# A hybrid SSD, attention and expert layer on one core: the SSD's mask, exponentials and products spread over steps, and the first LayerNorm done in halves

## The chip, the core and the metric

The kernel runs on one core of a Trainium2 chip. The metric is the device time of one execution in microseconds; the kernel before took 1722.3 us (median of three executions, 1720.65 to 1722.61). Shares and rows come from one profiled execution. The engines are TensorE (PE; its weight loads are PEld), VectorE (DVE), ScalarE (ACT), GpSimd (POOL) and SyncE (SP), which here issues most DMAs. Each works through its own queue in order.

## The reference, cut to what matters

512 rows of width 1024 pass through one decoder layer:

```python
h = layer_norm(x, ln_in_g, ln_in_b)
proj = h @ w_in                                   # z, xbc, dt, q_lat, kv_lat, k_pe
xbc = silu(causal_dwconv(xbc, conv_w, conv_b))    # 4 taps; then xs, B, C
seg = a_cum[..., :, None] - a_cum[..., None, :]
decay = exp(where(causal, seg, -inf))
y_diag = einsum('bcgels,bcsgep->bclgep', cb[:, :, :, None] * decay, xdt)
# states between chunks, y_off = C . prev . exp(a_cum), y += d_skip * xs, gate by silu(z)
# in parallel: latent attention of 8 heads; both @ w_out; LayerNorm; expert mixer; LayerNorm
```

There are 16 SSD heads of width 64 in two groups with a state of 128. The kernel works with chunks of 128 rows (c = 0 to 3), so that chunk and group (c, g) make eight pieces of eight heads, each a 128 x 8 x 128 tile of decays. All matrix products of the projections are made of three passes (high times high, high times low, low times high) of operands that are split into a high and a low half.

## The kernel before, in words

The order of all instructions is written by hand: what is issued first in the Python text stands first in its engine's queue. Buffers come from pools, and a tile that reuses a buffer makes its writer wait for the old readers.

**Weights.** `Stream` (L75 to L108) brings the weights as numbered items of 512 KB. `loads` issues a DMA on SP into one of three raw buffers `wir`; `splits` makes the high half `wih` on ScalarE (L99) and the low half `wil = wir - wih` (L100) on the engine that `lo` names, VectorE as a rule, and then issues the load three items on. `get(n)` splits up to item n + 2; there are three pairs of `wih` and `wil`. `proj(i)` (L294) takes item i and does 8 blocks k of three matmuls (`mm3`, L66 to L69) over 512 columns into a psA bank of PSUM. psA and psB have four banks each.

**First LayerNorm** (L228 to L280). The four row blocks of `XH` are loaded; statistics of all four, one `rsqrt` (a bit trick and three Newton steps on VectorE, L110), one scale `nm4`; the blocks are normalised by ScalarE and VectorE; then for each of eight column blocks k four transposes on TensorE into a bank, `ht` on ScalarE (gain and bias), the high half `HH` by a copy on VectorE and the low half `HL` on VectorE for even k and on GpSimd for odd k. Then `XH` times gain plus bias (L276, L277; the rows come by a broadcast DMA `rows`, L235) makes the residual, three blocks on GpSimd and one on VectorE, stored to `xsp` by DMAs of GpSimd's queue. The low half of item 0 is made on GpSimd too.

**Projections of the SSD** (L515 to L533). For i = 0 to 12: `proj(i)`; `conv_a` (ScalarE's copy `cu`, four VectorE steps into `ca`), a step later `conv_b` (SiLU on ScalarE), and two steps later `conv_c` (four transposes on TensorE, a copy on ScalarE; nothing for i = 3 and 4). The dt path (`dt_prep`) runs in pieces between; its last piece writes the cumulated decays `acT` to memory (`acd`), and `decay_rows(n)` reads them back by a broadcast DMA of GpSimd's queue into one of three `de` tiles, the next when `ssd_y` has used one. `k_rope` (i = 3) has two fp32 matmuls.

**SSD.** `ssd_a(c, g)` (L406): for g = 0 the product C·B of the chunk on TensorE, in a psB bank, and ScalarE's copy `cbT`; then the mask on VectorE (L415), eight exponentials on ScalarE (L418) and the product with `cbT` on VectorE (L419). `ssd_x(c)`: `xdt`, `xdw` and the skip product on VectorE. `ssd_off(c)`: two matmuls with the state, and on VectorE `yo` (L441) and its sum (L442). `ssd_y(c, g)`: 8 fp32 matmuls of 128 x 128 (L450) in two psB banks, emptied by VectorE sums (L454). `ssd_s(c)`: the state (L464, L461, L466). The table `work` puts these behind the projections 13 to 17 (q and kv latents, steps 0 to 4) and the eight gate items (z, L588, steps 5 to 12). `lat_a` and `lat_b` (L550, L563) normalise the latents: column sums, an `rsqrt` chain, a diagonal, a matmul, scales and splits.

**Attention** (from L765): `q_pe(0)` and `qk_nope(0)`, then three steps of `chain(qk_nope(1), v_proj(0))`, the third of which is the first half of `v_proj(0)`; then 38 steps `st` with scores, softmax, transposes and products, each taking one more step of the chain.

Behind it come the output projection, a LayerNorm, the expert scores, and the long expert stage (`ut` and `v` items) that takes most of the time. The change does not touch them.

Of the kernel before, what the change touches and what calls it, by code (L numbers as in the profile page):

```python
# [23 lines left out]
S = 512  # L24
# [24 lines left out]
def tile_block(ctx: ExitStack, tc: tile.TileContext, I, out):  # L49
# [119 lines left out]
    def rows(t, i):  # L169
        nc.sync.dma_start(t, bass.AP(tensor=I["rows"].tensor, offset=I["rows"].offset + i * D,  # L170
                                       ap=[[0, 128], [D, 2], [1, D]]))
# [51 lines left out]
    def item():  # L223
        cnt[0] += 1
        return win.get(cnt[0] - 1)
# [5 lines left out]
    win.loads(1)  # L231
# [10 lines left out]
    nc.sync.dma_start(iaE.rearrange("p a b -> p (a b)"), I["ch"][:, 256:512])  # L242

    V.memset(ones, 1.0)
    win.lo = lambda n: G if n == 0 else lo_on[0]
    win.splits(1)
    mv4 = lnp.tile([128, NB, 2], F32, name="mv4")
    ve4 = lnp.tile([128, NB], F32, name="ve4")
    for b in range(NB):
        st6 = lnp.tile([128, 2, 6], F32, name="st6", bufs=2)  # L250
        for i in range(2):
            V.bn_stats(st6[:, i], XH[:, b, i * 512:(i + 1) * 512])
        V.bn_aggr(mv4[:, b], st6.rearrange("p a b -> p (a b)"))
    V.tensor_scalar(ve4, mv4[:, :, 1], EPS, None, op0=OP.add)
    rs4 = rsqrt(lnp, ve4, [128, NB], "l0")
    nm4 = lnp.tile([128, NB], F32, name="nm4")
    V.scalar_tensor_tensor(nm4, mv4[:, :, 0], -1.0, rs4, op0=OP.mult, op1=OP.mult)
    for b, cs, act in ((0, slice(0, D), 0), (1, slice(0, D), 1), (2, slice(0, D), 0),
                       (3, slice(0, 512), 1), (3, slice(512, D), 0)):
        t = XH[:, b, cs]  # L260
        if act:
            A.activation(t, t, AF.Identity, bias=nm4[:, b:b + 1], scale=rs4[:, b:b + 1])
        else:
            V.tensor_scalar(t, t, rs4[:, b:b + 1], nm4[:, b:b + 1], op0=OP.mult, op1=OP.add)
    for k in range(8):
        ps = pa() if k % 2 else pb()
        for b in range(NB):
            T.transpose(ps[:, b * 128:(b + 1) * 128], XH[:, b, k * 128:(k + 1) * 128], ident)
        ht = lnp.tile([128, S], F32, name="ht", bufs=3)
        A.activation(ht, ps, AF.Identity, bias=PAR[:, P_LB + k:P_LB + k + 1], scale=PAR[:, P_LG + k:P_LG + k + 1])  # L270
        V.tensor_copy(HH[:, k], ht)
        (G if k % 2 else V).tensor_tensor(HL[:, k], ht, HH[:, k], op=OP.subtract)
    win.splits(3)
    for b in range(NB):
        E = V if b == 3 else G
        E.tensor_tensor(XH[:, b], XH[:, b], zt[:, 0], op=OP.mult)  # L276
# [14 lines left out]
    kpe = [lat.tile([128, S], F32R, name=f"kpe{i}") for i in range(2)]  # L291
    kd = wk.tile([128, S], F32, name="kd")

    def proj(i):  # L294
        h, l = item()
        h = h.rearrange("p (k c) -> p k c", k=8)
        l = l.rearrange("p (k c) -> p k c", k=8)
        ps = pa()
        for k in range(8):
            mm3(ps, h[:, k], l[:, k], HH[:, k], HL[:, k], k == 0, k == 7)  # L300
        return ps

    cu, co = {}, {}
# [51 lines left out]
    def dt_prep():  # L355
# [33 lines left out]
        for n in range(3):  # L389
            decay_rows(n)  # L390
        ps = pb()
        T.matmul(ps[:, 0:64], tri, af, start=True, stop=True)
# [13 lines left out]
    def ssd_a(c, g):  # L406
        sl = slice(c * 128, (c + 1) * 128)
        if g == 0:
            pc = pb()
            for e in range(2):  # L410
                T.matmul(pc[:, e * 128:(e + 1) * 128], bcT[:, e, sl], bcT[:, 2 + e, sl], start=True, stop=True)
            cbT = SD["cb"] = ssw.tile([128, 2, 128], F32, name="cbT")
            A.activation(cbT.rearrange("p a b -> p (a b)"), pc[:, :256], AF.Copy)
        de = de_[c * 2 + g]
        V.tensor_tensor(de, de, ntm[:, None, :].to_broadcast([128, 8, 128]), op=OP.add)  # L415
        for h in range(8):
            hh = g * 8 + h
            A.activation(de[:, h], de[:, h], AF.Exp, bias=nac[:, c, hh:hh + 1])  # L418
        V.tensor_tensor(de, de, SD["cb"][:, g:g + 1].to_broadcast([128, 8, 128]), op=OP.mult)  # L419

    def ssd_x(c):
        xdt = SD["xdt"] = ssw.tile([128, D], F32, name="xdt")
# [11 lines left out]
    def ssd_off(c):  # L434
        if c:
            for g in range(2):
                po = pb()
                T.matmul(po, bcT[:, 2 + g, c * 128:(c + 1) * 128], prev[0][:, g * 512:(g + 1) * 512],
                         start=True, stop=True)
                yo = ssw.tile([128, 512], F32, name="yo")  # L440
                V.tensor_tensor(hb(yo), hb(po), eac[:, c, g * 8:(g + 1) * 8, None].to_broadcast([128, 8, 64]), op=OP.mult)  # L441
                V.tensor_tensor(xs[g][:, c], xs[g][:, c], yo, op=OP.add)  # L442

    def ssd_y(c, g):
# [8 lines left out]
            yv = y[:, q % 2 * 256:(q % 2 + 1) * 256].rearrange("p (a b q) -> p a b q", a=2, b=2)  # L453
            V.tensor_tensor(yv, yv, pv, op=OP.add)  # L454
        del de_[c * 2 + g]
        decay_rows(c * 2 + g + 3)

    def ssd_s(c):
        nxt = ssw.tile([128, D], F32, name="prev", bufs=2)
# [82 lines left out]

# [876 lines left out]
```

## Time and profile before

| | |
|---|---|
| median of three executions | 1722.3 us |
| the profiled execution | 1720.65 us |
| its span, first to last instruction | 1718.9 us |
| TensorE busy | 1631.2 us (95%) |
| VectorE busy | 1373.3 us (80%) |
| ScalarE busy | 680.2 us (40%) |
| GpSimd busy | 484.5 us (28%) |
| TensorE clock granted, mean | 0.986 |

A row of the timeline has the start, the length, the engine, the line, the operation, output and inputs, and in brackets the idle time before it and what ended it. A row of the groups has the count (x8), then busy time and mean ns of one, then idle time before it. Matmuls overlap, so the distance of their starts, not their length, is the rate. A row of the windows has a stretch, its length, the busy time of PE, PEld, DVE, ACT and POOL, the granted clock (1.00 or 0.50 within one stretch), the DMA share and GB/s.

### The profile page before, as it was taken

Reading aid. Unit: us, or ns where it says so; the run is one execution under the profiler, and the core shown is the slowest. Engines: PE = TensorE matmul, PEld = TensorE weight load, DVE = VectorE, ACT = ScalarE, POOL = GpSimd, SP = SyncE. Lnnn points to the kernel's source line nnn. Section 1 sums busy time; section 2 is a strip of 40 time slices with the busy share of each in tenths; the row PEclk is TensorE's granted clock in tenths of the full one; section 3 lists DMA queues with packets and bytes.
Section 4 is the critical chain, followed back from the end, with each engine's and each line's share of the span. In section 5 each row is a group of like instructions: output and inputs, shape, how many; then the busy total and the mean of one; then the engine's idle time right before and its main releaser. Section 6 shows DMA issues by size and latency. Waiting matters only on the chain.

```text
span 1718.9 us, 23562 instructions
## 1 busy us (share of the span) xinstructions
PE 1631.2 (95%) x8639; PEld 1432.0 (83%) x8639; DVE 1373.3 (80%) x2659; ACT 680.2 (40%) x1072; POOL 484.5 (28%) x331
## 2 busy tenths in 40 slices
PE   5998899999899989999999999999999999999996
PEld 4776677878788989898989999999999999888884
DVE  8877678864639999999668778787788888898976
ACT  3463456652223333555433333333333333333331
POOL 5100000000033410000045455555444544643301
PEclk9999999999999999999999999999999999999998
DMA  5333111265322333666689999999999999999972
GB/s 193 115 112 109 51 51 42 79 228 158 121 77 86 99 99 122 233 221 233 235 304 334 321 344 330 317 335 336 340 308 346 334 318 332 348 348 335 335 219 100
DMA packets 145491, 384.66 MB, mean 224 GB/s; under 512 B 11856, under 2 KB 62032, under 8 KB 143456
## 3 DMA queue, kind: packets, MB, share of 16 engines
q1 hardware_dynamic: 104672, 236.85, 40.6%
q0 software_dynamic: 40416, 145.80, 23.6%
q8 instruction: 67, 1.10, 0.3%
q10 hardware_dynamic: 288, 0.52, 0.1%
q14 instruction: 48, 0.39, 0.1%
HBM read 350.59 MB, written 31.49 MB: 222 GB/s over the span
## 4 chain that ended last, share of the span: by engine, by line
PE 71%; DVE 19%; ACT 5%; issue 2%; DMA 1%; DVEq 0%; SPq 0%; ACTq 0%
PE va L1175 10%; PE va L1176 10%; PE va L1179 10%; PE pu L67 8%; PE pu L69 8%; PE pu L68 8%; DVE wil L100 3%; PE pa L67 2%; PE pa L68 2%; PE pa L69 2%; ACT wih L99 2%; PE pw L69 2%; PE pw L68 2%; PE pw L67 2%; DVE t L883 1%
## 5 line engine op out<-in xcount | busy, mean ns | idle before, releaser
L100 DVE TENSOR_TENSOR wil<-wir,wih 128x1024 fp32r<-128x1024 f32 (+3 forms) x314 | 378.9, 1208 | 207.2 <-ACT wih L99 204.3
L99 ACT ACTIVATE wih<-wir 128x1024 fp32r<-128x1024 f32 (+2 forms) x340 | 352.4, 1038 | 330.9 <-issue 162.3
L69 PE MATMUL pu<-XTH,wil 128*128 128x384 f32 x1008 | 341.4, 339 | 4.4 <-DVE wil L100 4.4
L67 PE MATMUL pu<-XTH,wih 128*128 128x384 f32 x1008 | 344.0, 341 | 1.0 <-ACT sc L869 1.0
L68 PE MATMUL pu<-XTL,wih 128*128 128x384 f32 x1008 | 340.9, 338 | 0.0
L1212 POOL DMA_INDIRECT row<-u,ix x128 | 190.6, 1489 | 434.8 <-DMA wir<-v 261.8
L1175 PE MATMUL va<-wih,Ph 128*128 128x512 f32 x768 | 300.5, 391 | 2.1 <-ACT Ph L1159 2.1
L1176 PE MATMUL va<-wil,Ph 128*128 128x512 f32 x768 | 300.5, 391 | 0.3 <-DVE wil L100 0.3
L1212 POOL DMA_INDIRECT row<-v,ix x128 | 183.6, 1434 | 202.0 <-DVE ac L1229 172.8
L1179 PE MATMUL va<-wih,Pl 128*128 128x512 f32 x768 | 239.4, 391 | 0.0
L1066 ACT ACTIVATE act<-pu 128x384 f32<-128x384 f32 x126 | 62.0, 492 | 366.8 <-PE pu L69 366.8
L69 PEld LDWEIGHTS pu<-XTH,wil 128*128 128x128 f32 x1008 | 189.1, 188 | 5.0 <-DVE wil L100 5.0
L67 PEld LDWEIGHTS pu<-XTH,wih 128*128 128x128 f32 x1008 | 189.1, 188 | 4.0 <-ACT sc L869 1.2
L68 PEld LDWEIGHTS pu<-XTL,wih 128*128 128x128 f32 x1008 | 189.3, 188 | 2.9
L1175 PEld LDWEIGHTS va<-wih,Ph 128*128 128x128 f32 x768 | 144.6, 188 | 31.7 <-ACT Ph L1159 2.8
L1179 PEld LDWEIGHTS va<-wih,Pl 128*128 128x128 f32 x768 | 144.4, 188 | 30.5 <-DVE Pl L1166 0.3
L1176 PEld LDWEIGHTS va<-wil,Ph 128*128 128x128 f32 x768 | 144.5, 188 | 28.9 <-DVE wil L100 0.7
L1229 DVE SCALAR_TENSOR_TENSOR ac<-row,hd,ac 128x1024 f32<-128x1024 f32 x128 | 164.1, 1282 | 2.3
L1223 DVE SCALAR_TENSOR_TENSOR row<-row,x 128x1024 f32<-128x1024 f32 x128 | 150.0, 1220 | 0.8 <-DMA row<-u,ix 0.8
L100 POOL TENSOR_TENSOR wil<-wir,wih 128x1024 fp32r<-128x1024 f32 x26 | 62.4, 2401 | 233.3 <-ACT wih L99 233.3
L1151 DVE TENSOR_TENSOR P<-act,gt 128x384 f32<-128x384 f32 x128 | 70.6, 552 | 6.4 <-DMA gt<-gsp 6.4
L1159 ACT ACTIVATE Ph<-P 128x384 fp32r<-128x384 f32 x128 | 65.9, 515 | 20.5 <-DVE P L1151 20.4
(397 smaller groups left out, 2494.6 us busy)
## 6 DMA issues: line engine op xcount, KB each, us to landing
wir<-ut SPq DMA_DIRECT2D x128, 512.0 KB
wir<-v SPq DMA_DIRECT2D x128, 512.0 KB
gsp<-stg SPq DMA_DIRECT2D x12, 2048.0 KB
gt<-gsp SPq DMA_DIRECT2D x32, 768.0 KB
wir<-wo SPq DMA_DIRECT2D x26, 512.0 KB
wir<-wf SPq DMA_DIRECT2D x18, 512.0 KB
wir<-wqr SPq DMA_DIRECT2D x16, 512.0 KB
de<-acd POOLq DMA_DIRECT2D x8, 512.0 KB
```

The lines of the kernel that those rows point to most:

```text
L67: T.matmul(ps, lh, rh, start=start, stop=False)
L68: T.matmul(ps, lh, rl, start=False, stop=False)
L69: T.matmul(ps, ll, rh, start=False, stop=stop)
L99: A.activation(h, r, AF.Copy)
L100: self.lo(n).tensor_tensor(l, r, h, op=OP.subtract)
L1151: V.tensor_tensor(P.rearrange("p (b t) -> p b t", t=32), a.rearrange("p (b t) -> p b t", t=32), gt[c // 4][:, :, c % 4, :], op=OP.mult)
L1175: T.matmul(va[b][e], Ph[:, bs], h[:, cs], start=c == 0, stop=False)
L1176: T.matmul(va[b][e], Ph[:, bs], l[:, cs], start=False, stop=False)
L1179: T.matmul(va[b][e], Pl[:, bs], h[:, cs], start=False, stop=c == 127)
L1212: G.indirect_dma_start(out=R[s], out_offset=None, in_=I["u"] if s < 128 else I["v"], in_offset=bass.IndirectOffsetOnAxis(ap=ix[:, s % 128: ...
L1223: V.scalar_tensor_tensor(r, r, 1.0, x3, op0=OP.mult, op1=OP.mult, accum_out=hd[:, s:s + 1])
L1229: V.scalar_tensor_tensor(ac, r, hd[:, s - 128:s - 127], ac, op0=OP.mult, op1=OP.add)
```

## The change

1. **LayerNorm in two halves.** Statistics, `rsqrt`, scale, normalising and transposes are done for blocks 0 and 1, then for 2 and 3, into eight open PSUM banks. ScalarE makes both blocks of the first half. Then per k: `ht` on ScalarE; `HH` on ScalarE from PSUM for odd k, on VectorE for even k; `HL` always on VectorE. The low half of item 0, and the residual of all four blocks, are on VectorE.
2. **Loads.** Items 0 to 2 are asked for earlier. The broadcast `rows` moves from the head of SP's queue to behind the split of item 1.
3. **Two projections in step.** Items 0 and 1 run block by block through two banks; `get` goes on with item 2.
4. **`conv_c` later** for the first ones: 1 at step 4, and 3 and 2 at step 5.
5. **SSD.** The mask becomes `ssd_m`, issued one place before the exponentials, and those one place before the sums that use them; `ssd_a` for g = 0, with the C·B product, now often stands right behind `ssd_y`. Four `de` tiles instead of three. `acT` and `yo` lose their own buffers and use the two `cu` buffers.
6. **Attention.** Two steps of the chain ahead of the loop instead of three.

```diff
-    rows(zt[:, 0:2], 0)
-
-    win.loads(2)
+    win.loads(3)
...
+    PS8 = [pa() if k < 4 else pb() for k in range(8)]
+    for p in range(2):
+        bs = slice(2 * p, 2 * p + 2)
...
+        rs = rsqrt(lnp, ve, [128, 2], "l0")
+        V.scalar_tensor_tensor(nm, mv4[:, bs, 0], -1.0, rs, op0=OP.mult, op1=OP.mult)
...
+        for k in range(8):
+            for b in (2 * p, 2 * p + 1):
+                T.transpose(PS8[k][:, b * 128:(b + 1) * 128], XH[:, b, k * 128:(k + 1) * 128], ident)
     win.splits(1)
...
+        A.activation(ht, PS8[k], AF.Identity, bias=pl, scale=pg)
+        if k % 2:
+            A.activation(HH[:, k], PS8[k], AF.Identity, bias=pl, scale=pg)
         else:
+            V.tensor_copy(HH[:, k], ht)
+        V.tensor_tensor(HL[:, k], ht, HH[:, k], op=OP.subtract)
+        if k == 0:
+            win.splits(2)
+            rows(zt[:, 0:2], 0)
     win.splits(3)
     for b in range(NB):
-        E = V if b == 3 else G
-        E.tensor_tensor(XH[:, b], XH[:, b], zt[:, 0], op=OP.mult)
-        E.tensor_tensor(XH[:, b], XH[:, b], zt[:, 1], op=OP.add)
+        V.tensor_tensor(XH[:, b], XH[:, b], zt[:, 0], op=OP.mult)
+        V.tensor_tensor(XH[:, b], XH[:, b], zt[:, 1], op=OP.add)
...
+    def proj_k(ps, hl, k):
+        h, l = (z.rearrange("p (k c) -> p k c", k=8)[:, k] for z in hl)
+        mm3(ps, h, l, HH[:, k], HL[:, k], k == 0, k == 7)
...
+                for k in range(8):
+                    for j in range(2):
+                        proj_k(two[j], win.w[j], k)
...
-            t = de_[n] = ssw.tile([128, 8, 128], F32, name="de", bufs=3)
+            t = de_[n] = ssw.tile([128, 8, 128], F32, name="de", bufs=4)
...
-        acT = ssw.tile([64, 128], F32, name="acT")
+        acT = wk.tile([128, S + 3], F32, name="cu", bufs=2)[0:64, 0:128]
...
-        V.tensor_tensor(de, de, ntm[:, None, :].to_broadcast([128, 8, 128]), op=OP.add)
...
+    def ssd_m(c, g):
+        de = de_[c * 2 + g]
+        V.tensor_tensor(de, de, ntm[:, None, :].to_broadcast([128, 8, 128]), op=OP.add)
...
-                yo = ssw.tile([128, 512], F32, name="yo")
+                yo = wk.tile([128, S + 3], F32, name="cu", bufs=2)[:, :512]
...
-        if i >= 3:
+        if i >= 5:
             conv_c(i - 2)
+        if i in (4, 5):
+            conv_c(i - 3)
...
+        if i == 11:
+            ssd_m(0, 0)
         if i == 12:
+            ssd_m(0, 1)
             ssd_a(0, 0)
...
-    work = {0: [(conv_c, 12), (ssd_x, 0)], 1: [(ssd_y, 0, 0), (ssd_y, 0, 1)],
-            2: [(ssd_s, 0), (ssd_a, 1, 0)], 3: [(ssd_a, 1, 1), (ssd_x, 1), (ssd_off, 1)],
-            4: [(ssd_y, 1, 0), (ssd_y, 1, 1)], 5: [(ssd_s, 1), (ssd_a, 2, 0)],
-            6: [(ssd_a, 2, 1), (ssd_x, 2), (ssd_off, 2)], 7: [(ssd_y, 2, 0), (ssd_y, 2, 1)],
-            8: [(ssd_s, 2), (ssd_a, 3, 0)], 9: [(ssd_a, 3, 1), (ssd_x, 3), (ssd_off, 3)],
+    work = {0: [(conv_c, 12), (ssd_x, 0), (ssd_m, 1, 0)],
+            1: [(ssd_y, 0, 0), (ssd_y, 0, 1), (ssd_a, 1, 0), (ssd_m, 1, 1)],
+            2: [(ssd_s, 0), (ssd_a, 1, 1), (ssd_m, 2, 0)], 3: [(ssd_x, 1), (ssd_off, 1), (ssd_m, 2, 1)],
+            4: [(ssd_y, 1, 0), (ssd_y, 1, 1), (ssd_a, 2, 0)], 5: [(ssd_s, 1), (ssd_a, 2, 1), (ssd_m, 3, 0)],
+            6: [(ssd_x, 2), (ssd_off, 2), (ssd_m, 3, 1)], 7: [(ssd_y, 2, 0), (ssd_y, 2, 1), (ssd_a, 3, 0)],
+            8: [(ssd_s, 2), (ssd_a, 3, 1)], 9: [(ssd_x, 3), (ssd_off, 3)],
             10: [(ssd_y, 3, 0), (gate, 0, 0)], 11: [(ssd_y, 3, 1), (gate, 1, 0), (gate, 2, 0)],
             12: [(gate, 3, 0)]}
...
-    for _ in range(3):
+    for _ in range(2):
         next(g)
```

More of the change, by code (lines that the diff above doesn't have):

```diff
@@ L230, in tile_block @@
     nc.sync.dma_start(PAR, I["fpar"])
-    win.loads(1)
+    win.loads(2)
     nc.sync.dma_start(CT, I["cst1"])
@@ L244, in tile_block @@
     V.memset(ones, 1.0)
-    win.lo = lambda n: G if n == 0 else lo_on[0]
-    win.splits(1)
[L247 to L262, printed above, removed]
-        else:
-            V.tensor_scalar(t, t, rs4[:, b:b + 1], nm4[:, b:b + 1], op0=OP.mult, op1=OP.add)
@@ L265, in tile_block @@
[L265 to L272, printed above, removed]
+    mv4 = lnp.tile([128, NB, 2], F32, name="mv4")
@@ new lines, in tile_block @@
+    PS8 = [pa() if k < 4 else pb() for k in range(8)]
+    for p in range(2):
+        bs = slice(2 * p, 2 * p + 2)
+        for b in (2 * p, 2 * p + 1):
+            st6 = lnp.tile([128, 2, 6], F32, name="st6", bufs=2)
+            for i in range(2):
+                V.bn_stats(st6[:, i], XH[:, b, i * 512:(i + 1) * 512])
+            V.bn_aggr(mv4[:, b], st6.rearrange("p a b -> p (a b)"))
+        ve = lnp.tile([128, 2], F32, name="ve", bufs=2)
+        nm = lnp.tile([128, 2], F32, name="nm", bufs=2)
+        V.tensor_scalar(ve, mv4[:, bs, 1], EPS, None, op0=OP.add)
+        rs = rsqrt(lnp, ve, [128, 2], "l0")
+        V.scalar_tensor_tensor(nm, mv4[:, bs, 0], -1.0, rs, op0=OP.mult, op1=OP.mult)
+        for j, cs, act in (((0, slice(0, D), 1), (1, slice(0, D), 1)) if p == 0 else
+                           ((0, slice(0, D), 0), (1, slice(0, 512), 1), (1, slice(512, D), 0))):
+            t = XH[:, 2 * p + j, cs]
+            if act:
+                A.activation(t, t, AF.Identity, bias=nm[:, j:j + 1], scale=rs[:, j:j + 1])
+            else:
+                V.tensor_scalar(t, t, rs[:, j:j + 1], nm[:, j:j + 1], op0=OP.mult, op1=OP.add)
+        for k in range(8):
+            for b in (2 * p, 2 * p + 1):
+                T.transpose(PS8[k][:, b * 128:(b + 1) * 128], XH[:, b, k * 128:(k + 1) * 128], ident)
@@ L292, in tile_block @@
     kd = wk.tile([128, S], F32, name="kd")
+    def proj_k(ps, hl, k):
+        h, l = (z.rearrange("p (k c) -> p k c", k=8)[:, k] for z in hl)
+        mm3(ps, h, l, HH[:, k], HL[:, k], k == 0, k == 7)
+    two = {}
     def proj(i):
-        h, l = item()
-        h = h.rearrange("p (k c) -> p k c", k=8)
-        l = l.rearrange("p (k c) -> p k c", k=8)
+        if i < 2:
+            if i == 0:
+                cnt[0] = 2
+                for j in range(2):
+                    two[j] = pa()
+                for k in range(8):
+                    for j in range(2):
+                        proj_k(two[j], win.w[j], k)
+            return two[i]
+        hl = item()
         ps = pa()
         for k in range(8):
-            mm3(ps, h[:, k], l[:, k], HH[:, k], HL[:, k], k == 0, k == 7)
+            proj_k(ps, hl, k)
         return ps
@@ L385, in dt_prep @@
         T.matmul(ps[0:64, 0:128], af, tri, start=True, stop=True)
-        acT = ssw.tile([64, 128], F32, name="acT")
+        acT = wk.tile([128, S + 3], F32, name="cu", bufs=2)[0:64, 0:128]
         A.activation(acT, ps[0:64, 0:128], AF.Copy)
         G.dma_start(acd, acT)
-        for n in range(3):
+        for n in range(4):
             decay_rows(n)
@@ L455, in ssd_y @@
         del de_[c * 2 + g]
-        decay_rows(c * 2 + g + 3)
+        decay_rows(c * 2 + g + 4)
     def ssd_s(c):
```

2 lines of the change are left out of this document (added).

## The prediction

> **What bounds the kernel now.** I read the page first, then the waits of TensorE in the stretch that the change touches (20 to 275 us), then the groups of VectorE from 110 to 232 us, then stretches with the granted clock.
>
> ```profile
> span 1718.9 us, 23562 instructions
> ...
> PE 71%; DVE 19%; ACT 5%; issue 2%; DMA 1%; DVEq 0%; SPq 0%; ACTq 0%
> ```
>
> TensorE carries 71% of the chain that ended last. The change leaves its matmuls alone, so it can only move the waits between them, and all of it lies ahead of 260 us. What it gains there shifts all that follows, since each later stage reads the one before.
>
> ```profile
> PE pb L450 <- ACT wih L99: 7.1, 1, 7.1
> PE pb L332 <- ACT bcT L323: 3.1, 1, 3.1
> PE pb L332 <- ACT co L323: 2.2, 2, 1.9
> PE pa L68 <- POOL HL L272: 2.2, 2, 1.5
> PE pt L735 <- DVE P L726: 2.1, 1, 2.1
> PE pb L450 <- ACT ca L580: 1.7, 1, 1.7
> PE pb L565 <- DVE xs L454: 1.6, 1, 1.6
> ...
> PE pb L450 <- issue: 1.5, 1, 1.5
> ...
> PE pb L450 <- DVE yo L441: 0.9, 2, 0.4
> ```
>
> These are all the TensorE waits worth naming: 5.3 us in LayerNorm and the first convolutions (L68, bcT), 15.0 us in the SSD (L450, L565, co), 2.1 us in the first attention step.
>
> ```profile
> L100 DVE TENSOR_TENSOR wil<-wir,wih 128x1024 fp32r<-128x1024 f32 x11 | 13.4, 1219 | 0.3 <-ACT wih L99 0.3
> L419 DVE TENSOR_TENSOR de<-de,cbT 128x1024 f32<-128x1024 f32 x8 | 9.8, 1225 | 21.7 <-ACT de L418 21.7
> ```
>
> VectorE stands still for 21.7 us in 110 to 232 us, each time between its mask (L415) and its product (L419), for eight exponentials. What TensorE waits for comes behind that.
>
> ```profile
> 47.37:50.78 3.41, 0.30 (x3) 0.31 (x4) 3.41 (x2) 0.99 (x2) 2.97 (x3) 1.00 0.04 16
> 50.78:57.61 6.83, 6.83 (x14) 3.47 (x13) 3.82 (x9) 2.19 (x4) 0.00 (x0) 0.50 0.65 224
> 115.64:119.05 3.41, 1.55 (x10) 1.05 (x9) 2.36 (x2) 3.38 (x8) 0.00 (x0) 1.00 0.00 0
> 119.05:122.46 3.41, 3.41 (x11) 2.64 (x10) 0.00 (x0) 3.40 (x9) 0.00 (x0) 0.50 0.00 0
> ```
>
> First column after the length is TensorE's busy time, the third from the right the clock. A stretch with 1.55 of 3.41 us busy is followed by 3.41 us at half clock, one with 0.30 busy by 6.83 us. Half clock over 3.41 us costs 1.7 us of matmuls.
>
> **A. LayerNorm, two projections, residual (to about 55 us).**
>
> ```profile
> 11.50 2.33 DVE L117 SCALAR_TENSOR_TENSOR l0a<-l0y 128x4 f32<-128x4 f32 x1
> ...
> 14.84 0.16 DVE L257 SCALAR_TENSOR_TENSOR nm<-mv,l0y 128x4 f32<-128x4 f32 x1
> ...
> 18.83 0.69 DVE L272 TENSOR_TENSOR HL<-ht,HH 128x512 fp32r<-128x512 f32 x1
> ```
> ```profile
> L270 ACT ACTIVATE ht<-pb,PAR 128x512 f32<-128x512 f32 x4 | 3.1, 779 | 1.9 <-POOL HL L272 1.3 <-PE pb L268 0.6
> ...
> L276 DVE TENSOR_TENSOR XH<-XH,zt 128x1024 f32<-128x1024 f32 x1 | 3.4, 3424 | 0.0
> ...
> L99 ACT ACTIVATE wih<-wir 128x1024 fp32r<-128x1024 f32 x6 | 6.2, 1052 | 8.3 <-DMA wir<-wf 8.3
> ```
>
> While GpSimd works, VectorE's 0.16 us step takes 2.33 and its 1024-wide one 3.42 instead of about 1.22 (L100 above). The change takes all GpSimd arithmetic out of here. The second `rsqrt` chain costs 13 more steps at 0.2 (13.83 to 14.84 holds five), 2.5 us, and saves that 2.2 us stall, so the last scale `nm` comes at 15.1 us, as now (14.84 + 0.16). From there ScalarE has 0.8 (half block), three splits at 1.05, and eight `ht` plus four `HH` at 0.78: 13.3 us, less about 0.08 of overlap per operation: done at 27.3. VectorE's share (per pair of blocks one cast and two differences of 0.69) fits beside it, and a matmul needs only its own block k.
>
> ```profile
> 150.44 0.39 PE L68 MATMUL pa<-HL,wih 128*128 128x512 f32 x1
> 150.66 0.39 PE L69 MATMUL pa<-HH,wil 128*128 128x512 f32 x1
> ```
>
> Matmuls start every 0.227 us. The two projections in step are held for the second block until HL1 (15.1 + 0.8 + 1.05 + 0.78 + 1.05 + 2 x 0.78 + 0.69, about 21.1); then 7 x 6 x 0.227 = 9.5: both end at 30.6, item 2 (24 x 0.227 = 5.45) at 36.0.
>
> Now the price. Eight residual steps stand on VectorE ahead of the first convolution and of the low half (wil) of item 3. They were never seen alone; bounds are 1.22 each (L100, two f32 operands, same size) and 3.42 (beside GpSimd). GpSimd is idle, so I take 1.22, 1.15 start to start.
>
> ```profile
> 51.46 0.55 DVE L312 TENSOR_SCALAR ca<-cu,PAR 128x512 f32<-128x512 f32 x1 [0.55 <-ACT wih L99]
> 52.04 2.33 DVE L314 SCALAR_TENSOR_TENSOR ca<-cu,PAR,ca 128x512 f32<-128x512 f32 x3
> ```
>
> 27.3 + 1.2 (wil of item 2) + 8 x 1.15 + 3.1 (convolution 1) + 1.2 = 42.0. TensorE, done with item 2 at 36.0, has the small dt transposes and item 3's first two matmuls (no wil in them) and then waits about 5.2 us: longer than the 3.1 us wait on bcT that the later `conv_c` removes. Item 3 then ends at 42.0 + 22 x 0.227 = 47.0.
>
> ```profile
> 50.48 0.86 PE L332 MATMUL pb<-ident,bcT 128*128 128x128 f32 x4 [3.14 <-ACT bcT L323]
> 51.27 2.07 PE L508 MATMUL pb<-kd,CT 64*128 64x512 f32 x2
> ...
> 54.98 0.79 PE L67 MATMUL pa<-HH,wih 128*128 128x512 f32 x1
> ```
>
> `k_rope` (51.27 to 54.98) takes 3.7 at half clock, 1.9 at full: item 4 at 48.9, plus 1.7 to 3.4 for the clock after so long a wait, say 2.6: 51.5. Now it starts at 54.98 and loses another 1.3 until 57.61. Gain 4.8; the moved transposes (0.86 at half clock) still have to be paid, 0.4. **A: -4.4**, from -7.0 (no half clock) to -3.6.
>
> **B. SSD (109 to 232 us).** In times of the present trace, up to item 12's end (109) nothing differs.
>
> ```profile
> 111.27 1.28 ACT L418 ACT_TABLE_LOAD   x1
> 114.09 2.45 ACT L418 ACTIVATE de<-de,nac 128x128 f32<-128x128 f32 x8 [1.54 <-DVE de L415]
> ```
>
> (1) The mask is done an item earlier, so these exponentials start 1.54 sooner; the co wait falls from 1.9 to 0.3 and its half-clock stretch (119.05) goes: 3.2 us. But ScalarE's queue, only 1.5 us ahead, now rules: the first `ssd_y` starts about 124.3 instead of 126.12.
>
> ```profile
> 126.12 3.74 PE L450 MATMUL pb<-xdt,de 128*128 128x128 f32 x32
> 129.61 0.48 PE L67 MATMUL pa<-HH,wih 128*128 128x512 f32 x1
> ```
> (2) A new wait. The next chunk's C·B product now stands right behind `ssd_y` and takes the fifth of four psB banks: it waits for the first L454, which stands in VectorE's queue behind xdt's second half, xdw, the skip products, a mask, a wil and a sum (0.6 + 1.15 + 1.2 + 1.15 + 1.15 + 0.65 = 5.9). TensorE ends `ssd_y` at 127.8, gets its bank at 130.5 and starts item 15 at 130.9, not 129.61. Everything on TensorE is queued behind this wait, and so are ScalarE's exponentials, behind the copy of that product.
>
> (3) From here VectorE no longer stands still in front of xdt. TensorE: item 15 to 136.4, chunk state 1.7, item 16 to 143.6, the sums of `lat_a` 0.8. VectorE (1.15 start to start for a 1024-wide step, 0.7 for a 512-wide one, as HL) gets its last exponentials of chunk 1 at 141.1 (behind ScalarE's copies of the state) and has product, mask and wil done at 144.6; then the rsqrt chain with its diagonal 2.4 + 0.9, xdt, xdw and skip 3.5, y_off 4 x 0.7, mask, wil and sum 2.9, and L454 of chunk 1 0.4: 157.5. The waits 1.7 + 1.5 + 0.9 + 1.6 become one of 2.5 (`ssd_y` ends at 154.9), and behind the product `lat_b` (L565) starts at 157.9.
>
> ```profile
> 160.55 0.70 PE L565 MATMUL pb<-co,ones 128*128 128x512 f32 x1 [1.57 <-DVE xs L454]
> ```
> ```profile
> 171.72 0.88 DVE L560 TENSOR_SCALAR co<-ident,lsy 128x128 f32<-128x128 f32 x4
> ```
>
> (4) From the product of chunk 2 (160.8) VectorE is the bound without a pause: product 1.2, `lat_b` 3 x 2.1 (two steps and ScalarE's copy between), wil 1.2, rsqrt and diagonal 3.3, state 2.5, product, mask and wil 3.5, `lat_b` 2 x 2.1, xdt, xdw and skip 3.5, y_off 2.9, mask and wil 2.3, L454 0.4 are 31.3 us, to 192.1. The 7.1 us wait splits into waits of 1.1, 0.8, 1.6, 1.8, 0.6 and 2.5, and the fourth gate item starts at 192.5, with chunk 3's product (0.4) already behind it. Now:
>
> ```profile
> 196.91 0.48 PE L67 MATMUL pa<-wih,HH 128*128 128x512 f32 x1
> ```
>
> Gain 196.91 - 192.5 + 0.4 = 4.8. After that neither kernel waits until 232 us. Against it: the new waits of 2.7 and 2.5 us leave stretches emptier than 115.64 did. If they fall so (I say 7 in 10), each costs 1.7: 2.4. (The one at 155 us would be hidden under VectorE.) **B: -2.4**, from -4.8 to +2.0 (two double stretches, 3.4 each).
>
> The Trainium skill ("TensorE: Matmul & The Clock Gate", section "HAM oscillation — how this bites in real kernels") states that only idle gaps above about 3.4 us throttle; by it B would be -4.8. The trace differs: waits of 3.14 and 1.85 us were throttled.
>
> **C. First attention steps.** `v_proj` is begun a step later.
>
> ```profile
> 247.61 0.60 ACT L637 ACTIVATE vh<-pu 128x512 fp32r<-128x512 f32 x1 [1.53 <-PE pu L69]
> ```
>
> The first exponential need no longer wait for the second half of v: 1.1 us sooner, but vl (0.69) then falls into the softmax chain. **C: -0.8**, from 0 to -2.1 (the whole L735 wait).
>
> At nothing I cost the fourth `de` buffer (its load goes out with the first three and is used a chunk later; wrong, it would hold mask and VectorE by its landing), the copies in `cu` slots (no convolution is left when `yo` takes one), and the residual's stores (earlier, on a POOL queue that is else idle).
>
> Sum: 4.4 + 2.4 + 0.8 = 7.6 off the profiled execution's 1720.65 (span 1718.9 and 1.75 around it): 1713.05. That execution is the fastest of three; the median stands 1.65 above it, so 1714.7.
>
> **Rivals.** *B gives nothing* (VectorE's queue order eats it; for it, the new bank waits; against, the 21.7 us that are filled): 1722.3 - 5.2 = 1717.1. *No new half clock in B* (for it, the new waits are shorter than the 3.14 that was throttled; against, 1.85 was too): 1714.7 - 2.4 = 1712.3; the Trainium skill's rule above is this case. *The clock takes it all*: every new wait, those at 37, 128, 155 and 190 us, is followed by 6.83 us at half clock as 47.37 was: A loses 0.8 more, B 3 x 3.4 - 2.4 = 7.8, C is nothing: 1714.7 + 9.4 = 1724.1, no change. *Slower: the gain and bias rows come late.*
>
> ```profile
> 7.33 0.33 SPq L170 DMA_DIRECT2D zt<-rows  x1
> ```
>
> This 1 MB load now stands on SP behind the loads of items 3 and 4, which wait for wil of items 0 and 1 (about 20.5 us). Up to 28.5 us it is hidden; then each us holds the residual steps, the in-order VectorE, item 3 and TensorE. From 36.1 it eats the whole gain, from 39.6 on the kernel is slower; at 41, 1727. Against it:
>
> ```profile
> 0.00:20.00 20.00, 4.09 (x17) 3.51 (x18) 13.63 (x32) 6.58 (x7) 2.60 (x6) 1.00 0.85 317
> ```
>
> At 317 GB/s, 1.5 MB take 5 us: 26.
>
> **Chances.** Forecast 0.52, no new half clock 0.2, B nothing 0.15, clock 0.08, rows late 0.05. A measurement tells about 0.2% (3.4 us) from no change. Faster (below 1718.9): 0.52 + 0.2 + 0.1 = 0.82; same: 0.08 + 0.05 = 0.13; slower 0.05. Range: down to 1708 (A -7.0, B -4.8, C -2.1), up to 1719.5 (A -3.6, B +0.8, C 0).
>
> **What would show it.** Right: no GpSimd arithmetic before 60 us, both first projections done near 31, a new TensorE wait on wil L100 of about 5 us near 37 to 42; the 21.7 us in front of the product nearly gone, new waits of about 2.6 us before the C·B products, each on L454 or its like. Wrong: residual steps well above 1.22 us, half clock after most new waits, or L450 still waiting 5 us or more.

## The result, and the profile after

| | before | after |
|---|---|---|
| median | 1722.45 us (1720.65 to 1723.21, 4 runs) | 1709.67 us (1709.52 to 1710.38, 4 runs) |
| profiled execution | 1720.65 us | 1709.54 us |
| its span | 1718.9 us | 1707.6 us |

The ratio is 0.9928 (95% interval 0.9911 to 0.9945): 12.8 us faster, where 7.6 was forecast. Profile against profile it is 11.1 us. First the page, then the waits of TensorE from 20 to 232 us (total, times, longest):

```profile
span 1707.6 us, 23555 instructions
...
PE 71%; DVE 20%; ACT 5%; issue 2%; DMA 1%; DVEq 0%; SPq 0%; ACTq 0%
```
```profile
PE pb L430 <- DVE xs L476: 6.6, 3, 2.4
PE pa L69 <- DVE wil L100: 4.8, 1, 4.8
PE pb L472 <- issue: 2.8, 2, 1.7
PE pb L472 <- DVE xdt L448: 1.3, 1, 1.3
PE pb L460 <- DVE prev L488: 0.8, 1, 0.8
PE pb L351 <- ACT co L342: 0.7, 2, 0.4
```

The chain has the same owners as before. The 7.1 us wait on wih and the 3.1 on bcT are gone, and the two new kinds that the forecast named stand on top: the C·B product (L430) three times on a bank that L476 must free, and item 3 on its low half (L100).

To place the gain I set the same instruction of both kernels side by side on TensorE: the C·B product of chunk 0 (before, then after), the start of the latent attention (MLA, the first product of `q_pe`), and a softmax scale (VectorE) well inside the attention.

```profile
109.56 0.61 PE L411 MATMUL pb<-bcT 128*128 128x128 f32 x4
...
236.02 1.02 PE L653 MATMUL pu<-qx,C 128*128 128x512 f32 x2
...
317.98 0.49 DVE L726 TENSOR_SCALAR P<-P,sm 128x512 f32<-128x512 f32 x1
```
```profile
104.70 0.61 PE L430 MATMUL pb<-bcT 128*128 128x128 f32 x4
...
226.48 1.02 PE L681 MATMUL pu<-qx,C 128*128 128x512 f32 x2
...
307.61 0.49 DVE L754 TENSOR_SCALAR P<-P,sm 128x512 f32<-128x512 f32 x1
```

| part | forecast | measured |
|---|---|---|
| A, to 109 us | -4.4 | 109.56 to 104.70: -4.86 |
| B, to the start of MLA | -2.4 | -9.54 in all: -4.68 |
| C, first attention steps | -0.8 | -10.37 in all: -0.83 |
| behind it | 0 | span -11.26 in all: -0.9 |

A and C came as forecast; B brought twice as much; the last 0.9 comes in a part of the code that is the same in both. In the windows of the kernel before there is a stretch at half clock (0.50) that the changed one does not have at that place, and half of 3.41 us is 1.7:

```profile
368.23:371.64 3.41, 1.50 (x8) 0.91 (x7) 1.99 (x3) 2.49 (x3) 0.00 (x0) 1.00 0.61 208
371.64:375.05 3.41, 3.41 (x9) 2.65 (x10) 0.97 (x1) 0.00 (x0) 0.00 (x0) 0.50 0.96 297
```

Windows of the changed kernel, around the wait on wil and around the first wait on L476:

```profile
35.78:39.19 3.41, 1.24 (x8) 0.62 (x6) 3.20 (x6) 1.88 (x2) 0.80 (x2) 1.00 0.38 154
39.19:46.02 6.83, 4.18 (x10) 3.31 (x11) 6.57 (x10) 1.58 (x2) 0.00 (x0) 0.50 0.61 203
121.10:124.51 3.41, 2.15 (x20) 1.96 (x18) 3.41 (x5) 0.00 (x0) 1.05 (x2) 1.00 0.51 169
124.51:127.93 3.42, 2.27 (x12) 1.96 (x13) 2.09 (x6) 1.52 (x6) 0.00 (x0) 1.00 0.81 241
...
46.02:247.41 201.39, 184.99 (x895) 146.61 (x893) 146.96 (x261) 103.42 (x204) 5.85 (x11) 1.00 0.26 83
```

The wait on wil draws 6.83 us at half clock, as forecast; 4.18 us of them have matmuls, so about 2 us are lost. None of the three new SSD waits draws any: the clock stays at 1.00 from 46.02 to 247.41.

### The profile page after: what moved, and what is told of

It reads as the page before. It is cut to its first block, busy times and chain, and to the rows that moved or that the text cites. A ratio compares the mean times of both kernels' runs of the same rounds, so it can differ in the third digit from the quotient of the medians.

```text
span 1707.6 us, 23555 instructions
## 1 busy us (share of the span) xinstructions
PE 1625.9 (95%) x8639; PEld 1427.6 (84%) x8639; DVE 1364.7 (80%) x2678; ACT 682.7 (40%) x1077; POOL 458.6 (27%) x320
## 4 chain that ended last, share of the span: by engine, by line
PE 71%; DVE 20%; ACT 5%; issue 2%; DMA 1%; DVEq 0%; SPq 0%; ACTq 0%
PE va L1204 10%; PE va L1203 10%; PE va L1207 10%; PE pu L67 8%; PE pu L69 8%; PE pu L68 8%; DVE wil L100 3%; PE pa L69 2%; PE pa L67 2%; PE pa L68 2%; PE pw L69 2%; PE pw L68 2%; PE pw L67 2%; ACT wih L99 1%; DVE t L911 1%
## 5 line engine op out<-in xcount | busy, mean ns | idle before, releaser
L100 DVE TENSOR_TENSOR wil<-wir,wih 128x1024 fp32r<-128x1024 f32 (+2 forms) x315 | 376.8, 1198 | 209.1 <-ACT wih L99 206.6
L100 POOL TENSOR_TENSOR wil<-wir,wih 128x1024 fp32r<-128x1024 f32 x25 | 60.0, 2401 | 221.0 <-ACT wih L99 221.0
```

What stands on the lines that cost most here:

```text
L100: self.lo(n).tensor_tensor(l, r, h, op=OP.subtract)
```

## The experiments

My theory of the extra 2.3 us of B: the new waits are as long as forecast, but whether one draws a half-clock stretch depends on where it falls in the clock's 3.41 us stretches (the phase of the clock, for short), so the 2.4 us that I charged were the wrong size. The rival is that B saved more waiting than I counted. For A, the theory was that the residual on VectorE is what TensorE waits for. Times are compared with the kernel before on the same chip.

**e1_ln_alone and e2_ssd_alone: the parts by themselves.** The first is the changed kernel with old SSD order and attention, the second the kernel before with these lines:

```diff
+    def ssd_m(c, g):
+        de = de_[c * 2 + g]
+        V.tensor_tensor(de, de, ntm[:, None, :].to_broadcast([128, 8, 128]), op=OP.add)
...
+            1: [(ssd_y, 0, 0), (ssd_y, 0, 1), (ssd_a, 1, 0), (ssd_m, 1, 1)],
...
+            t = de_[n] = ssw.tile([128, 8, 128], F32, name="de", bufs=4)
```

> Part A alone (LayerNorm in halves, two projections in step, residual on VectorE, later conv_c); SSD order and attention as before. Theory (the gains of the parts add, what is left is read from the trace): item 12 ends 4.9 us sooner (110.17 to 105.3), the SSD keeps its 15 us of waits, the whole is 4.9 us shorter: 1717.5 beside 1722.4. Rival (part A's gain hangs on the SSD behind it, or on the clock's stretches falling otherwise): item 12 as said, but the whole shorter by 3 us or less, or by 7 or more, with the difference in half-clock stretches behind 110 us.

> Part B alone (masks, exponentials and products a step apart, four row buffers, the two borrowed buffers); everything ahead of 110 us and the attention as before. Theory 1 (the new waits of 2.1 to 2.4 us stay too short for the clock in this order as well): the start of MLA comes 4.7 us sooner than 237.0, the whole is 4.7 us shorter, 1717.7, and no half clock between 119 and 232 us. Rival, the forecast's step (each new wait draws a half-clock stretch, and in the changed kernel they escaped by where the stretches of the clock happened to begin): one or two stretches at 0.50 behind the waits, each 1.7 us: 3.0 or 1.3 us shorter, 1719.4 to 1721.1.

Measured: A alone 1714.73 against 1721.19 us (0.9957, 0.9941 to 0.9973), B alone 1716.96 (0.9981, 0.9969 to 0.9993). The interval of B alone allows 1.2 to 5.3 us, so its time holds both theories, and its median lies nearer to theory 1 (1717.7); the trace has to decide. By position, A alone leads by 3.86 us at item 8 (4.86 in the changed kernel: here 6.06 us of matmuls fall into the half clock behind the wait on wil, there 4.18), and by only 3.13 at the end of the gate items; there B alone leads by 1.12, having stood 0.41 behind at item 8, so its SSD gains 1.53, not 4.68. Yet the waits of B alone are the same as in the changed kernel:

```profile
PE pb L411 <- DVE xs L457: 6.6, 3, 2.4
```

What differs is the clock:

```profile
127.36:130.77 3.41, 1.15 (x11) 0.96 (x9) 3.41 (x5) 0.00 (x0) 0.74 (x2) 1.00 0.60 208
130.77:134.18 3.41, 3.25 (x10) 2.77 (x11) 1.10 (x4) 1.99 (x7) 0.00 (x0) 0.50 0.73 247
192.21:195.62 3.41, 1.49 (x9) 1.32 (x10) 2.86 (x6) 0.68 (x3) 0.00 (x0) 1.00 0.23 65
195.62:199.03 3.41, 3.41 (x10) 2.67 (x9) 1.35 (x2) 3.39 (x9) 0.00 (x0) 0.50 0.22 89
```

Two half-clock stretches, behind the first and the third new wait, about 1.6 us each: 3.15 us is what the SSD's gain lacks. For B the rival (the forecast's step) holds in this trace. In A alone the old SSD order is slower by 0.7 and has 13.66 us at half clock in the SSD (windows 153.81 to 160.64 and 184.53 to 191.36) where the kernel before has 10.24. The whole of A alone came 6.5 us shorter, between the two theories' bounds; the times do not decide there, positions do. Behind the start of MLA, in code that is the same, the spans of both runs gain some 3 us more; the kernel before has 17.1 us at half clock there, these runs 13.7, which explains about half of it, and the rest is open.

**e6_busy_wait: fill the wait on wil.**

```diff
+        if i == 3:
+            pd = pb()
+            for n in range(21):
+                T.matmul(pd, HH[:, 0, 0:128], HH[:, n % 8], start=n == 0, stop=n == 20)
```

> The changed kernel with 21 extra matmuls of 128x512 (HH by HH, result not used) ahead of projection item 3, to fill TensorE's 4.8 us wait on wil L100. Theory (the wait costs twice: itself, and then 2.2 us at half clock, item 3 taking 7.2 us instead of 5.0): the wait is filled and gone from the waits, the half clock of 39.19 to 46.02 goes, item 4 starts 2.2 us sooner (48.7), the whole is 1.6 to 2.2 us shorter than the changed kernel, 1707.5 to 1708. Rival (item 3 is slow for another reason, its operands still come late): item 4 at 50.9 as now, no gain, 1709.7.

Measured: 1707.99 us (0.9916, 0.9902 to 0.9931). Starts of item 4 after and in this run (PE):

```profile
41.84 0.80 PE L69 MATMUL pa<-HH,wil 128*128 128x512 f32 x1 [4.82 <-DVE wil L100]
...
50.89 0.50 PE L67 MATMUL pa<-HH,wih 128*128 128x512 f32 x1
```
```profile
36.23 5.08 PE L541 MATMUL pb<-HH 128*128 128x512 f32 x21
...
48.94 0.50 PE L67 MATMUL pa<-HH,wih 128*128 128x512 f32 x1
...
123.72 1.00 PE L430 MATMUL pb<-bcT 128*128 128x128 f32 x4 [2.42 <-DVE xs L476]
```

Item 4 starts 1.95 us sooner only because TensorE did work of no use meanwhile: that is the price of the half clock, 2.2 in the theory. The median hits the theory's 1707.5 to 1708. The profiled execution (1709.32, the slowest of six) does not: at the end of the gate items just 0.3 of the 1.95 is left. The wait before the C·B product has the same 2.42 us as in the changed kernel (2.41), and here it is throttled:

```profile
120.58:123.99 3.41, 0.99 (x9) 0.81 (x8) 3.41 (x6) 0.00 (x0) 0.53 (x1) 1.00 0.67 259
123.99:127.40 3.41, 3.41 (x11) 2.83 (x11) 0.67 (x3) 2.65 (x10) 0.00 (x0) 0.50 0.66 202
```

Here the wait (121.30 to 123.72) lies within one stretch, which has 0.99 us of work left in it; in the changed kernel it lay across the border at 124.51, and both stretches kept more than 2.1 us. Same wait, same code around it, 1.6 us apart. Together with B alone, that shows the theory of B.

**e5_again: the changed kernel unchanged.**

> The changed kernel itself once more, for another phase of the clock's 3.41 us stretches (so far the first record began at 15.3 us after the first instruction in the changed kernel, at 16.4, 17.3 and 18.2 in others). Theory (half clock behind a new wait is decided by how the wait lies in those stretches): work and waits on the other engines as in the first trace within 0.1 us, and the stretches at 0.50 differ with the phase; the SSD's gain to the start of MLA is 4.7 us less 1.7 for each stretch that falls there, the time between 1706 and 1713. Rival (no phase: the program's own order decides): again no half clock between 47 and 247 us, and 1709.7.

Measured: 1709.72 us (1707.7 to 1711.4, five runs; 0.9931, 0.9911 to 0.9951). The first record of the clock began 15.61 us after the first instruction, only 0.3 from the first profile's, and again no half clock fell into the SSD; up to 340 us all positions agree within 0.15 us. As the phase hardly moved, this run decides nothing between the two theories.

**e11_gp_res: the residual of three row blocks back on GpSimd.**

```diff
+        E = V if b == 3 else G
-        V.tensor_tensor(XH[:, b], XH[:, b], zt[:, 0], op=OP.mult)
+        E.tensor_tensor(XH[:, b], XH[:, b], zt[:, 0], op=OP.mult)
```

> The changed kernel with the residual of row blocks 0 to 2 on GpSimd, as in the kernel before. Theory (GpSimd's arithmetic stretches VectorE's steps from 1.2 to 3.4 us, so it was right to take it away, although VectorE then has six steps more): wil of item 3 comes at about 48 instead of 41.8 us, item 4 5 to 7 us later, the whole 1715 to 1717. Rival (the engines do not hinder each other, the order does): six steps less on VectorE, wil of item 3 at about 35, the 4.8 us wait and its half clock gone, the whole 1703 to 1704.

Measured: 1715.5 us (0.9980, 0.9968 to 0.9991). VectorE in the changed kernel, and in this run:

```profile
27.96 1.22 DVE L282 TENSOR_TENSOR XH<-XH,zt 128x1024 f32<-128x1024 f32 x1
...
36.40 1.23 DVE L283 TENSOR_TENSOR XH<-XH,zt 128x1024 f32<-128x1024 f32 x1
...
38.32 2.33 DVE L333 SCALAR_TENSOR_TENSOR ca<-cu,PAR,ca 128x512 f32<-128x512 f32 x3
40.57 2.35 DVE L100 TENSOR_TENSOR wil<-wir,wih 128x1024 fp32r<-128x1024 f32 x2
```
```profile
29.79 3.42 DVE L283 TENSOR_TENSOR XH<-XH,zt 128x1024 f32<-128x1024 f32 x1
...
39.21 6.26 DVE L334 SCALAR_TENSOR_TENSOR ca<-cu,PAR,ca 128x512 f32<-128x512 f32 x3
45.40 2.35 DVE L100 TENSOR_TENSOR wil<-wir,wih 128x1024 fp32r<-128x1024 f32 x2
```

With six steps fewer VectorE is later, by 4.8 us: beside GpSimd its residual step takes 3.42 instead of 1.22 and the convolution 6.26 instead of 2.33. The wait on wil grows to 9.7 us and the kernel loses 5.8. The theory holds, if a little under its size: wil comes at 46.6, not 48.

**e7_wil_first and e10_no_step: two ways to the wait on wil.** One puts the splits of items 3 and 4 ahead of most of the residual, the other undoes the two projections in step:

```diff
     for b in range(NB):
+        if b == 1:
+            win.splits(5)
         V.tensor_tensor(XH[:, b], XH[:, b], zt[:, 0], op=OP.mult)
```
```diff
     def proj(i):
-        if i < 2:
+        if i < 0:
```

> The changed kernel with the splits of items 3 and 4 moved ahead of the residual of row blocks 1 to 3 on VectorE. Theory (the eight residual steps ahead of wil of item 3 are what TensorE waits for, and the half clock comes of that wait): the 4.8 us wait and the 6.8 us at 0.50 go, item 4 starts 6 to 7 us sooner (44 to 45 instead of 50.9), the whole is 6 to 7 us shorter than the changed kernel, 1703 to 1704. Rival (convolution 1 and the next splits, now behind, become late in their turn): a new TensorE wait of 3 us or more before 60 us and a gain of 3 us or less, 1707 or more.

> The changed kernel without the two projections in step: item 0 runs alone through its 8 blocks, then item 1. Theory (what two in step gains is lost again in the wait on wil L100 of item 3, which VectorE's residual steps set): item 2 ends 2 to 3 us later than 36.0, the 4.8 us wait shrinks to 2 to 3, item 3's last matmuls and item 4 come as now (50.9) or, where the shorter wait draws less half clock, up to 3 us sooner; the whole within 0.5 us of 1709.7, or shorter. Rival (part A's gain is the two in step): item 4 later by 2 to 3 us, the whole 1712 to 1713.

Measured: 1703.56 us (0.9898, 0.9875 to 0.9921) and 1704.0 us (0.9906, 0.9886 to 0.9926). The splits on VectorE with wil first (two of them, then the residual goes on), and without the step:

```profile
30.59 2.36 DVE L100 TENSOR_TENSOR wil<-wir,wih 128x1024 fp32r<-128x1024 f32 x2 [0.36 <-ACT wih L99]
32.87 1.22 DVE L284 TENSOR_TENSOR XH<-XH,zt 128x1024 f32<-128x1024 f32 x1
```
```profile
37.64 1.22 DVE L100 TENSOR_TENSOR wil<-wir,wih 128x1024 fp32r<-128x1024 f32 x1
38.80 0.06 DVE L328 MEMSET cu<- 128x3 f32 x1
38.97 0.55 DVE L331 TENSOR_SCALAR ca<-cu,PAR 128x512 f32<-128x512 f32 x1
```

The wait and the 6.83 us at half clock are gone in both. Item 4 starts at 43.68 and at 46.22 us, 7.2 and 4.7 sooner than at 50.89, and nearly all of it lasts to the end (the spans are 6.8 and 4.5 us shorter). The second is the surprise: at most 3 us sooner was expected. Two in step does what it should: item 2 comes 2.34 us sooner than without. But item 1 then no longer asks for its successors: `get` goes on with item 2, so the split of item 3 is issued behind convolution 1 (40.57) instead of ahead of it (37.64). TensorE arrives sooner and its operand later. The 2.34 us are paid back with 4.8 of waiting and 2.2 at half clock.

**e4_cb_early: the C·B product ahead of the sums.**

```diff
+    def ssd_p(c):
+        sl = slice(c * 128, (c + 1) * 128)
+        pc = pb()
...
+        A.activation(cbT.rearrange("p a b -> p (a b)"), pc[:, :256], AF.Copy)
...
-    work = {0: [(conv_c, 12), (ssd_x, 0), (ssd_m, 1, 0)],
+    work = {0: [(conv_c, 12), (ssd_x, 0), (ssd_p, 1), (ssd_m, 1, 0)],
```

> The changed kernel with the C.B product of chunks 1 to 3 and its copy issued at the end of steps 0, 3 and 6, ahead of ssd_y instead of behind it. Theory (the 6.6 us wait on the fifth bank is real time of the path, since VectorE then stands idle 2.6 us three times for the exponentials): the first and the third wait go, the second stays because lat_b's matmul takes the fifth bank in its place: 4.5 to 5 us shorter than the changed kernel, about 1705. Rival 1 (VectorE is the bound, so the waits move to ssd_y's xdt and de): within 1 us of 1709.7. Rival 2 (the copy cbT, one buffer, now waits on ScalarE for VectorE's product of the chunk before and holds the copies of the projections behind it): longer by 1 to 3 us.

Measured: 1699.92 us (0.9875, 0.9859 to 0.9890), 9.8 us below the changed kernel. No other edit brought as much. The same goes for steps 3 and 6 (chunks 2 and 3); `ssd_a` keeps the exponentials and the product with `cbT`. Waits from 105 to 232 us:

```profile
PE pb L473 <- DVE cu L464: 1.8, 2, 1.6
PE pb L595 <- DVE xs L477: 1.6, 1, 1.6
PE pb L351 <- ACT co L342: 0.7, 2, 0.4
PE pb L473 <- PE pa L69: 0.7, 1, 0.7
```

The L430 waits are gone, and lat_b's matmul (L595) takes the fifth bank as expected. The theory was right in kind and too small: the SSD's waits fall from 12.8 to 5.2 us, since ScalarE, which stood behind the copy of that product, begins its exponentials sooner (124.08 instead of 126.69 for chunk 1), and the waits behind them shrink too. From the C·B product of chunk 0 to the start of MLA the run takes 113.12 us, the changed kernel 121.77, neither with half clock there: 8.65 us less. At the end of the gate items it leads by 8.15; the other 1.2 come later, 0.8 of them in a TensorE wait on VectorE behind the attention (1.9 us in the changed kernel, 1.1 here).

**e8_cb_lat, e9_all_three and e12_cb_wil: added together.** The first moves lat_b of the q latent behind the first gate item, the second adds the early splits to it, the third is early product and early splits alone.

```diff
+        if n == 0:
+            lat_b(15)
             lat_a(17)
```

> The changed kernel with the early C.B products, and lat_b of the q latent moved one item later, behind the first gate item. Theory (the 1.6 us wait of lat_b's matmul on the fifth bank, L595 on L477 in the run with the early product alone, is real): that wait goes, and the whole is 1 to 1.6 us shorter than with the early product alone, 1698.3 to 1699. Rival (VectorE's queue, busy without a pause there, is the bound): the wait goes and comes back at the next ssd_y, 1699.9.

> All three edits together: early C.B products, lat_b of the q latent an item later, splits of items 3 and 4 ahead of most of the residual. Theory (the stages are apart, gains add): 9.8 + 0 to 1.6 + 6 to 7 us shorter than the changed kernel: 1691.5 to 1694. Rival (the earlier start meets VectorE's backlog or another phase of the clock): 1695 to 1699.

> The changed kernel with the early C.B products and the splits of items 3 and 4 ahead of most of the residual; lat_b stays where it is. Theory (the gains 9.8 and 6.8 add, the later lat_b gives nothing because VectorE is the bound there): no half clock ahead of 240 us, z's first SiLU at about 176 us, the whole 1691 to 1693. Rival (the run with all three was better for the later lat_b too): 1694 to 1695.

Measured: 1701.7 (0.9891, 0.9867 to 0.9914), 1693.11 (0.9846, 0.9825 to 0.9867) and 1695.15 us (0.9859, 0.9842 to 0.9877). The later lat_b gives nothing: its wait goes, but VectorE has the kv latent's diagonal ready later, lat_b of that one waits 1.4 us for it (0.4 in the changed kernel), and z's last SiLU is 1.2 us later in the run with all three (208.41) than in the one without it (207.20). From the C·B product of chunk 0 to the start of MLA the runs with the later lat_b take 114.33 and 114.36 us, both runs without it 113.12. That is the rival in kind: the wait comes back, if at lat_b and not at `ssd_y`. The other two add: 15.7 us ahead of the changed kernel at the end of the gate items, where the single gains are 8.15 and 7.26. In time the two versions can't be told apart (1695.15 is also what the rival of the last run said, so only the positions speak for its theory); both are some 14 to 17 us below the changed kernel, 1.4 to 1.5% below the one before.

**e3_attn_alone: the attention alone.**

```diff
-    for _ in range(3):
+    for _ in range(2):
```

> Part C alone: two steps of the chain ahead of the attention loop instead of three, on the kernel before. Theory (the forecast's term C, as read in the changed kernel): the first exponential 1.1 us sooner, from the fifth P on 0.8 us sooner, the whole 0.8 us shorter, below what the times can tell; the trace decides. Rival (the half of v_proj that is put off is late in the first step, and its low half is in the softmax chain): 0 or later by up to 0.7 us.

Measured: 1720.0 against 1719.46 us (0.9999, 0.9988 to 1.0010), no difference that times could show. In the trace:

```profile
238.59 1.02 PE L653 MATMUL pu<-qx,C 128*128 128x512 f32 x2
...
319.75 0.49 DVE L726 TENSOR_SCALAR P<-P,sm 128x512 f32<-128x512 f32 x1
```

From the start of MLA to this scale it takes 81.16 us, 81.96 in the kernel before (236.02 to 317.98): 0.80 us, and 81.13 in the changed kernel. The run also shows the size of the clock's chance: up to 238.59 its instructions are those of the kernel before, which is there at 236.02, 2.57 us sooner.

```profile
50.39:60.63 10.24, 9.75 (x20) 5.82 (x21) 6.74 (x13) 2.98 (x5) 0.65 (x2) 0.50 0.51 170
159.62:166.45 6.83, 6.02 (x16) 4.21 (x16) 4.96 (x10) 0.63 (x1) 0.54 (x1) 0.50 0.46 163
190.34:197.17 6.83, 3.81 (x17) 3.66 (x18) 5.67 (x8) 4.24 (x7) 0.00 (x0) 0.50 0.00 0
```

These are 23.9 us at half clock; the kernel before has 17.1 there (6.83, 3.41, 6.83).

## Why the prediction was right, and where it was off

**A** was right in its sum (-4.4, measured -4.86) and nearly in every time: nm at 14.9 to 15.1 us (15.1), the residual steps 1.22 us each as for a VectorE that shares with nobody, the wait on wil 4.82 (5.2), wil of item 3 ready at 41.8 (42.0), item 4 at 50.89 (51.5), the half clock 2 us (2.6). e11 shows that the reason for 1.22 was right, e6 the price of the clock. That the sum is met within half a microsecond is in part luck: by phase alone A gained 1.0 us less in e1, and the kernel before stood 1.76 us later at this place in e3. The forecast has the split of item 3 behind convolution 1 in its sum; what it did not see is that the two in step put it there, and that A without them would have gained 4.7 us more (e10).

**B** missed in one term. The waits came as forecast, 2.41, 2.09 and 2.11 us where "new waits of 2.7 and 2.5" stood, and the gain without the clock was to be 4.8 (measured 4.68). Step (4) was right as well: from the product of chunk 2 (156.32) to the end of the first sum behind it (187.3) VectorE has no pauses but those of `lat_b`, 31.0 us where the forecast added up 31.3. The term that missed is "If they fall so (I say 7 in 10), each costs 1.7: 2.4": nothing of it came. The price is right, as the time from the C·B product of chunk 0 to the start of MLA shows in all profiles with one SSD order or the other:

| SSD order | profiles | us at half clock there | us taken |
|---|---|---|---|
| before | before | 10.24 | 126.46 |
| before | e1, e3 | 13.66 | 127.2, 127.3 |
| changed | after, e5, e7, e10, e11 | 0 | 121.7 to 121.8 |
| changed | e6 | 3.41 | 123.38 |
| changed | e2 | 6.83 | 124.92 |

In the changed order each throttled wait costs 1.6 us. The table also shows what the gain of 4.68 is made of: TensorE's waits in the SSD only fell from 15.0 to 12.8 us, while the kernel before has 10.24 us at half clock, some 6.8 of them with matmuls, and the changed kernel has none. The larger part is the clock.

In these seven profiles of the changed order 3 of 21 such waits were throttled. That does not make the chance of 7 in 10 wrong. What decides is how much work is left in a 3.41 us stretch (last section): a wait of 2.4 us across a border leaves enough in both. If the clock's stretches are laid over the recorded work of the changed kernel at every possible phase, 0.64, 0.55 and 0.63 of the phases leave less than 1.6 us in one stretch at the three waits; this is an estimate from its trace. And the 21 are not 21 draws: in the changed kernel the three waits begin 27.5 and 34.5 us apart, nearly 8 and 10 stretches (27.3 and 34.1), so they fall at about the same place of a stretch, and in the five profiles without half clock the first one begins 1.7 to 2.2 us into its stretch. So the forecast charged a fair chance, and the phase made it nothing; that is luck. Whether something in the program favours this phase, no run shows.

The Trainium skill ("TensorE: Matmul & The Clock Gate", section "HAM oscillation — how this bites in real kernels") gives the rule of no TensorE idle gaps above about 3.4 us. By it B would have been -4.8, near the measured -4.68, but the runs contradict it: a wait of 2.42 us was throttled in e6. The same page, section "What's actually happening", says that the window of 3413 ns runs free of the kernel; the traces agree, since the stretches of 3.41 us begin at another place in each profile (the first clock record 15.3 to 21.5 us after the first instruction).

**The sign that "the 21.7 us in front of the product" would be "nearly gone"** was wrong. VectorE in 105 to 225 us:

```profile
L437 DVE TENSOR_TENSOR de<-de,cbT 128x1024 f32<-128x1024 f32 x8 | 9.8, 1225 | 19.6 <-ACT de L436 19.6
```

Still 19.6 us idle. Of the eight pauses only two became much shorter, the one in front of chunk 0's first product (2.52 to 0.99 us) and the one in front of chunk 2's second (2.51 to none); with the latter the 7.1 us wait ahead of chunk 2's sums became several short ones. That most of the idle time remained was a sign of what e4 then took: ScalarE's exponentials stood behind the product that waited for a bank. In e4 the pauses in front of the first product of chunks 1 to 3 (2.6 us each) are gone.

**C** was right (-0.8; -0.83 in the changed kernel, -0.80 alone). **The rivals**: the rows were not late (the residual began at 27.96, right behind wil of item 2, and GpSimd, which waits for them in e11, began at 26.14, where the forecast said 26), no wait took back B, and "no new half clock in B" is what the profile shows (0.2 in the forecast). With it the forecast was 1712.3; the 2.6 us from there to 1709.7 are 0.5 of A, 0.9 from the clock behind 370 us, and the way from the profiled execution to the median: I added 1.65, where the after profile stands 0.1 below its median. That last part is not settled further: 18 runs of the kernel before lay between 1716.8 and 1724.6 us.

## What to carry to other kernels

A wait for a PSUM bank can cost more than its length when another engine's work is queued behind the product that waits (6.6 us of such waits were worth 8.65 here): issue a small product before the ones that use up the banks. When a step is made to run sooner, look at what it used to trigger on its way; here the split of the next weights went behind a convolution and took back three times the gain. Count half clock from the work left in each 3.41 us stretch, as a chance, and compare two profiles by the positions of the same instructions, with the clock beside them.

## What the runs showed of the hardware

The clock falls to 0.50 behind a 3.41 us stretch with little work. Laid out in such stretches from its first clock record, the fourteen profiles have 68 at full clock with less than 1.55 us of TensorE work, and all 68 are followed by half clock; of the 6682 with 1.62 us or more none is; of the seven between, five are. (The ends of matmuls are modelled, so the border is good to some hundredths.) The emptiest stretch at one of the new SSD waits that kept its clock is in e7:

```profile
114.31:117.73 3.42, 1.72 (x16) 1.53 (x14) 3.42 (x5) 0.00 (x0) 1.05 (x2) 1.00 0.46 162
117.73:121.14 3.41, 2.69 (x14) 2.33 (x15) 1.66 (x5) 1.94 (x7) 0.00 (x0) 1.00 0.80 244
```

In the run with the later lat_b two short waits, 1.41 and 0.80 us, were enough together:

```profile
163.31:166.72 3.41, 1.45 (x3) 0.60 (x4) 3.24 (x8) 0.51 (x1) 0.00 (x0) 1.00 0.00 0
166.72:170.13 3.41, 3.41 (x7) 1.46 (x6) 3.41 (x4) 0.00 (x0) 0.00 (x0) 0.50 0.00 0
```

There it did not show in the time: this run and the one with all three edits, which has no half clock in the SSD, take 114.33 and 114.36 us from the C·B product of chunk 0 to the start of MLA. Elsewhere the same code took 1.6 us more at each throttled wait, by the clock's phase; that was as much as several of the edits here are worth.
